# An exchange of partition quarters through DRAM by four scattered writes and one contiguous read, with new order tables

## The chip, the cores and the metric

The kernel runs on one core of a Trainium2 chip. The metric is the device time of one launch in microseconds (us), the median of several runs. The core's engines are TensorE (PE: matmuls and transposes), VectorE (DVE), ScalarE (ACT), GpSimd (POOL) and SyncE (SP), which here only issues transfers (DMAs). Each engine works through its own instructions in a fixed order and waits where an operand or a buffer isn't ready; whatever stands behind a waiting instruction on that engine waits too, transfers on SP's queue included.

## The reference

One layer of a hybrid decoder on x of 512 positions by 1,024 features, all in float32: a normalised input is projected, three head groups (a gated delta rule, a diagonal state-space mixer called S5, and differential attention) work on it, one projection joins them, and a gated MLP with a short convolution follows. The change concerns the transfers of the S5 group; the new orders concern all of it.

```python
h = rms_norm(x, attn_norm_w)
g_q, g_k, g_v, g_z, g_b, g_a, s_u, d_q, d_k, d_v = split_cols(h @ w_in, IN_SIZES)
o_gdn = gated_delta_chunked(l2norm(g_q), l2norm(g_k), g_v, beta, log_decay)   # 4 heads, chunks of 64
o_s5 = rms_norm(s5_mixer(s_u, ...), s5_norm_w)     # 32 groups, 64 complex states, scan over positions, GELU, GLU
o_diff = diff_attention(d_q, d_k, d_v, lam)        # 4 heads, two causal softmax maps each
x = x + concat([o_gdn * silu(g_z), o_s5, o_diff]) @ w_out
x = x + (silu(gate) * up) @ w_down                 # gate, up = causal_dwconv(rms_norm(x) @ w_up)
out = rms_norm(x, final_norm_w)
```

## The kernel before

The features lie on the 128 partitions in eight tiles, the positions along the row. A weight matrix comes as blocks of 256 KB (`wblock`, line 550): a transfer into `wraw`, a cast on ScalarE to the rounded part `whi` (line 566), a subtraction on VectorE to the rest `wlo`. There are three buffers of each, so the transfer of a block waits until the `wlo` of the block three before it is written. Every product is three matmuls (rounded by rounded, rounded by rest, rest by rounded; `mm3`), accumulated in one of two PSUM banks `acc`. A bank is free again when ScalarE or VectorE has copied the result out; for the values of the attention that is the copy `dv` (line 1252), one for each half of the positions.

The order of TensorE's work is written out by hand in a string. The orders of VectorE, ScalarE, GpSimd and the issuing queue are four tables of numbers (`SEQUENCE`), which `in_order` ties into chains: number k is the k-th instruction of that engine in the order in which the program creates them.

The S5 group works in four parts. For part i, `s5_in` computes the input `up`, and `swap` (line 691) exchanges quarters of the partitions with quarters of the row, so that `u4` holds 32 positions in each quarter of the partitions; `s5_back` makes the output `yu` (VectorE, with a GELU whose tanh is on ScalarE) and exchanges it back into `yf`. So there are eight exchanges, called u0 to u3 and y0 to y3 here. An exchange is one transfer that writes the tile (256 KB, rows of 2 KB) to a DRAM tile `m` as it is, and four transfers of 64 KB that read a quarter of the partitions each, in pieces of 512 B. `yh` (line 812, ScalarE) and `yl` (VectorE) split `yf` for a later product; they are not urgent themselves, but stand in their engines' orders among the weight casts.

Other names in what follows: `gg` (VectorE, line 269) is the log decay of the delta rule, `cs`, `ct`, `z`, `zt` are the rotations and sums around the S5 scan, `en`, `wn`, `d` and `ff` tables and small blocks for matmuls, `kq` and `thc` the short convolution and its SiLU for the delta rule, `t_`, `f_`, `xc`, `lct` the steps of its triangular inverse (each `f_` a transpose of 32 by 32 blocks on VectorE, copied to `ff` by ScalarE). In the attention `dsm` is the row maximum (a reduction, line 1309) and the sums, `pp` the two probability maps and their difference, `qa`, `ka`, `kl` split queries and keys.

Of the kernel before, what the change touches and what calls it, by code (L numbers as in the profile page):

```python
# [59 lines left out]
226 172 244 173 219 174 222 175 243 176 223 177 246 178 224 179 254 180 201 181 225 182 202 183 228 184 203 185 227  # L60
186 229 187 230 188 272 277 231 122 233 123-124 232 125 210-211 234 212 235 304 213-214 256 236 306 257 305 269 215
258 237 259-262 273 263 274 264 275 265 311 266 276 267 239 268 238 240 307 293 292 296 309 294 310 295 328 297 312
332 308 313 247 314 248 250 249 298 324 251 315 325 327 326 316 329 333 252 279 278 280-281 334 299 301 300 282 335
302 330 303 284 283 336 318-319 285 320 337 286 364 321-322 331 365 287 323 288 290 289 291 366 353 352 355-356 354
357 367 359 358 338-341 379 360 255 361-362 342 381 363 344 343 374 368 373 345 369 375 346 270 376-377 271 347 378
348 350 370 349 351 371 396 413 389 388 391 390 192 196 392 193 197 393 414 317 194 380 416 382 372 384 383 419 394
397 395 385-386 398-400 415 401-403 405 404 406-407 420 408-409 411 410 412 424-425 417 387 418 461 421 426 463 422
460 462 427-429 434 423 435 440 430-432 441 433 436-437 458 438-439 442 459 443 456 455 457 444-448 468 449-452 477
453 464 454 469 482 465 470 466 471 467 472 476 473-475 487 498 478-480 483 481 500 484 488 485 489 486 490 493
491-492 494 503 495-497 506 499 511 501-502 522 504-505 507 538 509 508 512 542 510 544 513 516 514-515 541 517-518  # L70
521 519-520 543 548 523-525 533 527 529 531 539 534 553 545 535 540 536 526 546 528 537 547 530 532 560 549-550 554
551 555-556 552 561 587 557 588 558-559 579 563 580-582 564 577 576 578 583 565 562 566-569 584 601 570 585-586
571-572 589 573 598 574 603 575 593 590 600 591 594 592 595 597 599 609 596 602 610 604 614 605-607 615 608 612-613
611 616 623 619 617-618 620-622 628 641 624-627 642 629-633 651 637-638 634 639 635-636 652 640 643 669 668 670 653
647 644 671 648 645 649 654 646 650 657-658 655-656 663 659 664 660-662 693 665-667 672 674 694 675 673 696 677-678
691 690 697 679 692 680-683 676 684 695 713 685-687 719 688-689 698-699 703-704 700-702 734 705 714 709-710 706 711
707-708 712 715 735 720-722 716-718 729 723 727-728 730 724-726 731-733 738 736 739-740 737 742 744 741 748 743 754
745-747 759 749-750 752 751 753 763 755 757 756 758 765 760-762 769 764 772 766 768 767 775 770 778 771 773 781 776
784 779 787 782 790 785 794 788 774 791 777 793 780 783 800 786 789 792 801 795 802 1121-1122 796-799 1123 810 1124
803 1125-1126 804 806 811 815 805 807 816 808 1127-1128 812 821-822 813 809 814 817 826 818-819 827 823 832 820  # L80
# [11 lines left out]
1110 1115 1112 1117 1114 1119 1116 1118 1120 1129-1147 1149 1148 1153 1150-1151 1154-1155 1152 1156-1158  # L92
""",
    "scalar": """
0-1 3 2 5 4 6-24 27 25 29 33 26 28 51 30 44 31 46 34-35 43 52 45 36 39 49 37 40 38 41-42 57 32 50 53 55-56 92 97
58-59 54 62-64 60 65-66 61 67 69-76 68 77-81 86-87 82-85 108 93-94 88-89 102-104 47 95 110 105-106 90 48 91 107 96
121 123 109 98 111-114 99-101 115-117 124-125 122 118 126 150-151 131-132 127-128 146 137-139 129 119 140 144 130
141 120 142 147 145 148-149 133-136 168 143 174 152-154 158 156 189 159 190-191 155 192 157 160-161 164 166 165 162
186 169 167 170-173 197-202 175 212 163 176 214 178 177 179 183 185 180 184 187 181 193-194 188 195-196 204-207 203
215 208-211 182 222-223 220 213 257 216 259 217 225 221 218 256 258 226 228 224 229 232 227 219 233 236 230 237 231  # L100
# [51 lines left out]
def hybrid_trunk(ctx: ExitStack, tc: tile.TileContext, I: dict, out: bass.AP):  # L152
    nc = tc.nc
# [19 lines left out]
    dma = nc.sync.dma_start  # L173
# [1666 lines left out]
```

## Time and profile before

| | us |
|---|---|
| Median of 3 runs | 829.7 (827.82 to 830.31) |
| Profiled execution | 831.47 |
| Span of its trace, first to last instruction | 829.3 |
| TensorE busy | 792.8 |
| VectorE busy | 561.9 |
| ScalarE busy | 430.8 |
| GpSimd busy | 104.4 |

The mean granted clock of TensorE is 0.972 of the full one. In a timeline row the first number is the start, the second the time from the start to the end of what the row merges (xN instructions, whose pipelined times overlap a little), then engine, line, operation, result and operands, and in brackets how long the engine had been idle and what released it. A line such as L182 or L263 is a helper's that issues all matmuls or all tensor operations, so the names of the tiles tell the places apart.

### The profile page before, as it was taken

The numbers are of one execution on the slowest core, as the hardware profiler recorded it, in microseconds if no ns is written. First come the engines' busy times: TensorE is split into PE (matmuls) and PEld (weight loads), VectorE is DVE, ScalarE is ACT, GpSimd is POOL, SyncE is SP. The second block draws the span as 40 slices with busy tenths as digits, with TensorE's granted clock in tenths as the row PEclk, the third lists the DMA queues.
The fourth block names the chain that finished last, engine by engine and source line by source line (L and its number), as shares of the span: only waits on it lengthen the run. The fifth ranks groups of instructions, "written<-read, shape, count | busy, mean of one in ns | idle before, by whom it ended". The sixth has DMA issues, their size and how long they took to land.

```text
span 829.3 us, 13695 instructions
## 1 busy us (share of the span) xinstructions
PE 792.8 (96%) x5004; PEld 653.9 (79%) x5004; DVE 561.9 (68%) x1159; ACT 430.8 (52%) x1001; POOL 104.4 (13%) x133
## 2 busy tenths in 40 slices
PE   6979989998999999999999999999999999999996
PEld 6868877986777878787777788788888888888885
DVE  8998898754757866548447976766557656657634
ACT  5266356644567966675547644344244334335423
POOL 5710000000001210010003211011001001001101
PEclk8998999998998999999989999999999999999998
DMA  6856453378383633341214532333333333333202
GB/s 158 102 94 51 92 77 87 61 111 61 81 45 53 44 67 72 94 70 55 84 44 125 182 100 83 107 102 90 101 90 101 102 89 102 95 96 100 78 1 102
DMA packets 133562, 71.58 MB, mean 86 GB/s; under 512 B 12766, under 2 KB 129784, under 8 KB 133496
## 3 DMA queue, kind: packets, MB, share of 16 engines
q1 hardware_dynamic: 133496, 70.72, 40.6%
q8 instruction: 39, 0.64, 0.3%
q14 instruction: 27, 0.22, 0.1%
HBM read 66.51 MB, written 4.19 MB: 85 GB/s over the span
## 4 chain that ended last, share of the span: by engine, by line
PE 74%; DVE 11%; DMA 6%; ACT 4%; issue 2%; POOL 1%; SPq 1%; POOLq 0%; DVEq 0%; ACTq 0%
PE acc L182 62%; PE gp L182 5%; PE sp L182 4%; DMA wraw<-in_w_in_dram 4%; DVE wlo L263 2%; DVE kq L269 1%; PE sp L185 1%; DVE z L263 1%; PE gp L185 1%; DMA yf<-swap 1%; ACT whi L566 1%; DVE ct L263 1%; DVE z L662 1%; ACT gm L1022 1%; DVE zt L263 0%
## 5 line engine op out<-in xcount | busy, mean ns | idle before, releaser
L566 ACT CAST whi<-wraw 128x512 fp32r<-128x512 f32 (+2 forms) x224 | 133.2, 597 | 169.1 <-PE acc L182 142.5
L182 PE MATMUL acc<-h,whi 128*128 128x512 f32 x704 | 217.7, 390 | 0.0
L263 DVE TENSOR_TENSOR wlo<-wraw,whi 128x512 fp32r<-128x512 f32 (+2 forms) x224 | 151.7, 680 | 55.7 <-ACT whi L566 49.9
L182 PE MATMUL acc<-hT,whi 128*128 128x512 f32 (+1 forms) x464 | 154.2, 409 | 4.7 <-ACT dv L1252 2.9
L182 PEld LDWEIGHTS acc<-h,whi 128*128 128x128 f32 x704 | 132.1, 188 | 28.6 <-DVE h L269 0.6
L182 PE MATMUL acc<-h,wlo 128*128 128x512 f32 x352 | 137.0, 390 | 0.0
L182 PEld LDWEIGHTS acc<-hT,whi 128*128 128x128 f32 x464 | 88.6, 198 | 20.6 <-ACT dv L1252 3.1
L182 PE MATMUL acc<-hT,wlo 128*128 128x512 f32 (+1 forms) x240 | 92.6, 398 | 0.0
L263 DVE TENSOR_TENSOR x<-x,acc 128x512 f32<-128x512 f32 (+1 forms) x65 | 44.0, 677 | 57.3 <-PE acc L182 57.3
L182 PEld LDWEIGHTS acc<-h,wlo 128*128 128x128 f32 x352 | 66.1, 188 | 14.0 <-DVE wlo L263 0.3
L269 DVE SCALAR_TENSOR_TENSOR ac<-us,rt,ac 128x511 f32<-128x511 f32 x88 | 65.9, 750 | 12.9 <-ACT ac L1719 11.5
L263 POOL TENSOR_TENSOR ac<-ac 128x512 f32<-128x512 f32 x22 | 35.6, 1619 | 280.5 <-DVE ac L269 161.3
L182 PE MATMUL acc<-ah,whi 128*128 128x512 f32 x144 | 57.6, 400 | 0.1
L182 PE MATMUL acc<-ah,wlo 128*128 128x512 f32 x144 | 56.5, 392 | 0.0
L182 PE MATMUL acc<-al,whi 128*128 128x512 f32 x144 | 56.0, 389 | 0.0
L401 POOL TENSOR_TENSOR rs<-ms,expo 128x4 f32<-128x4 f32 (+1 forms) x14 | 19.3, 1375 | 278.8 <-DVE ms L400 274.6
L182 PEld LDWEIGHTS acc<-hT,wlo 128*128 128x128 f32 x240 | 46.4, 198 | 7.5
L263 DVE TENSOR_TENSOR us<-acc,rb 128x512 f32<-128x512 f32 x44 | 30.3, 688 | 27.9 <-PE acc L182 27.9
L1719 ACT ACTIVATE ac<-us,rt 128x512 f32<-128x512 f32 x44 | 36.0, 817 | 21.5 <-DVE us L263 21.5
L263 DVE TENSOR_TENSOR al<-ac,ah 128x512 fp32r<-128x512 f32 x22 | 15.2, 691 | 28.1 <-ACT ah L1733 27.5
L182 PEld LDWEIGHTS acc<-ah,whi 128*128 128x128 f32 x144 | 27.1, 188 | 6.7 <-issue 1.1
L1733 ACT CAST ah<-ac 128x512 fp32r<-128x512 f32 x22 | 13.7, 622 | 35.8 <-POOL ac L263 35.8
(567 smaller groups left out, 1404.2 us busy)
## 6 DMA issues: line engine op xcount, KB each, us to landing
wraw<-in_ffn_w_up_dram SPq DMA_DIRECT2D x88, 256.0 KB
wraw<-in_w_in_dram SPq DMA_DIRECT2D x64, 256.0 KB
wraw<-in_ffn_w_down_dram SPq DMA_DIRECT2D x32, 256.0 KB
wraw<-in_w_out_dram SPq DMA_DIRECT2D x24, 128.0 KB
xt<-in_x_dram SPq DMA_DIRECT2D x4, 512.0 KB
xj<-in_x_dram SPq DMA_DIRECT2D x8, 256.0 KB
wraw<-in_w_out_dram SPq DMA_DIRECT2D x8, 256.0 KB
lwraw<-in_ffn_w_down_dram SPq DMA_DIRECT2D x8, 256.0 KB
```

The lines of the kernel that those rows point to most:

```text
L182: pe(T.matmul(o, l, r, start=start, stop=stop))
L185: pe(T.transpose(o, i, ident_))
L263: e.tensor_tensor(o, a, b, op=op)
L269: e.scalar_tensor_tensor(o, a, s, b, op0=op0, op1=op1, **kw)
L401: ins = G.tensor_tensor(rs[:, :n], ms[:, :n], expo[:, :n], op=ALU.pow)
L566: S.copy(hi[:, :n], raw[:, :n])
L662: V.tensor_tensor_scan(zf[j], rr, zf[j], 0.0, ALU.mult, ALU.add)
L1022: S.activation(gm[:, n, :], m_ge, AF.Copy, scale=gp[:, n, h : h + 1])
L1719: S.activation(a, us, AF.Identity, scale=fcw(2, f), bias=fcb(f))
L1733: S.copy(ah[:, j, :], up)
```

## The change

`swap` writes four times, each time a quarter of the partitions into its place in every one of the 128 rows of `m` (pieces of 512 B), and then reads the whole of `m` in one transfer of 256 KB with rows of 2 KB. It is still five transfers per exchange, on the same queue. The four tables of `SEQUENCE` are new; TensorE's order is unchanged. Every line behind `swap` is one line further down in the new file.

```diff
     "sync": """
-9-12 14-15 13 16-17 19-23 32-33 40 34 57 41 58 35 42 59 36 38 43 37 39 44 26-29 60 24-25 30-31 61-62 47 52 63-64
+9-12 14-15 13 16-17 19-23 32-33 40 34 41 57-58 35 42 59 36 38 43 37 39 44 26-29 60 24-25 30-31 61-62 47-50 63 52-53
...
     def swap(o, x, n):
 
         m = dr.tile([P, 4, P], F32, name=f"swap{n}")
-        dma(m, x)
-        for b in range(4):
-            dma(o[32 * b : 32 * b + 32], m.rearrange("(a j) b c -> b j a c", j=32)[b])
+        v = m.rearrange("(b j) a c -> a j b c", j=32)
+        for a in range(4):
+            nc.sync.dma_start(v[a], x[32 * a : 32 * a + 32])
+        nc.sync.dma_start(o, m)
```

The issuing queue around the exchange y0 (`swap4`, from `yu` to `yf`) and u2 (`swap2`, from `up` to `u4`), before:

```order
L694 DMA swap4_1321<-yu_1319 128x512
L564 DMA wraw_1608<-in_w_in_dram 128x4x128
L696 DMA yf_124<-swap4_1321 32x4x128 x4
L694 DMA swap2_1452<-up_1449 128x512
L564 DMA wraw_1626<-in_w_in_dram 128x4x128
L696 DMA u4_1450<-swap2_1452 32x4x128 x4
L564 DMA wraw_1715<-in_w_in_dram 128x4x128
```

and now:

```order
L696 DMA swap4_1321<-yu_1319 32x4x128 x4
L564 DMA wraw_1608<-in_w_in_dram 128x4x128
L697 DMA yf_124<-swap4_1321 128x512
L696 DMA swap2_1452<-up_1449 32x4x128 x2
L564 DMA wraw_1626<-in_w_in_dram 128x4x128
L696 DMA swap2_1452<-up_1449 32x4x128 x2
L564 DMA wraw_1715<-in_w_in_dram 128x4x128
L697 DMA u4_1450<-swap2_1452 128x512
```

The four reads of y0 are one, behind the same weight block; u2 has its four writes around a weight block, and its read behind one more block.

ScalarE from the copies `wt` on, in the stretch that holds the first copy of `dv`, before:

```order
L742 COPY wt_1561<-sp_1560 128x512
L742 COPY wt_1568<-sp_1567 128x512
L1160 COPY ff_538<-f__1437 32x4x32
L773 COPY d00_120<-sp_1574 128x4x32
L775 COPY d00_120<-sp_1574 32x4x32 x2
L1252 COPY dv0_1458<-acc_1459 128x512
L790 COPY enx_116<-en_1329 64x32x16
```

and now:

```order
L743 COPY wt_1561<-sp_1560 128x512
L743 COPY wt_1568<-sp_1567 128x512
L1253 COPY dv0_1458<-acc_1459 128x512
L774 COPY d00_120<-sp_1574 128x4x32
L776 COPY d00_120<-sp_1574 32x4x32 x2
L566 CAST whi_1716<-wraw_1715 128x512
L1253 COPY dv0_1458<-acc_1460 128x512
```

The copy of `acc_1459` stands ahead of the `d00` copies, and the `ff` copy has gone from here (it now stands some ten rows further back).

VectorE in the attention's third and fourth blocks of rows, with a step of the triangular inverse (`xc`, `t__3441`, `f__3442`) between, before:

```order
L1110 STREAM_TRANSPOSE xc_3443<-lct_3436 128x128
L1309 TENSOR_REDUCE dsm_3545<-sp2_3546 128x2
L263 TENSOR_TENSOR xc_3443<-xc_3443,levs_511 128x128
L263 TENSOR_TENSOR kl0_3652<-dqk_2502,ka0_3646 64x512
L263 TENSOR_TENSOR t__3441<-ic_531,xc_3443 128x128
L263 TENSOR_TENSOR wlo_3706<-wraw_3704,whi_3705 128x512
L1110 STREAM_TRANSPOSE f__3442<-t__3441 128x128
L263 TENSOR_TENSOR xc_3584<-gp_3567,levs_511 128x128
L1314 RECIPROCAL dsm_3545<-dsm_3545 128x2
```

and now:

```order
L1111 STREAM_TRANSPOSE xc_3443<-lct_3436 128x128
L263 TENSOR_TENSOR xc_3443<-xc_3443,levs_511 128x128
L263 TENSOR_TENSOR t__3441<-ic_531,xc_3443 128x128
L1310 TENSOR_REDUCE dsm_3545<-sp2_3546 128x2
L1111 STREAM_TRANSPOSE f__3442<-t__3441 128x128
L263 TENSOR_TENSOR xc_3584<-gp_3567,levs_511 128x128
L263 TENSOR_TENSOR kl0_3652<-dqk_2502,ka0_3646 64x512
L263 TENSOR_TENSOR qa0_3644<-dqk_2502,qa0_3644 64x512
L263 TENSOR_TENSOR t__3610<-t__3441,gp_3593 128x128
L263 TENSOR_TENSOR qa1_3645<-dqk_2502,qa1_3645 64x512
L1315 RECIPROCAL dsm_3545<-dsm_3545 128x2
```

The reduction and `kl0` stand behind `t__3441`, and `wlo_3706` further back; two `qa` rows have come in.

The tables also move these: on VectorE two products `z` go behind `gg`, one `wlo` comes ahead of it; two sums `z` go behind `yu` of y1; two `qa` rows and one `wlo` come ahead of `yu` of y3. On ScalarE the tanh of y3 goes behind two `qa` casts and a weight cast. On the issuing queue one more weight block stands ahead of the exchange y3.

## Rows read from the trace of the kernel before

**Rows 1.** The page's first part: engine, busy us, share of the span, instructions

```profile
PE 792.8 (96%) x5004; PEld 653.9 (79%) x5004; DVE 561.9 (68%) x1159; ACT 430.8 (52%) x1001; POOL 104.4 (13%) x133
```

**Rows 2.** The page's fourth part: the chain that ended last, by engine

```profile
PE 74%; DVE 11%; DMA 6%; ACT 4%; issue 2%; POOL 1%; SPq 1%; POOLq 0%; DVEq 0%; ACTq 0%
```

**Rows 3.** TensorE's waits, 0 to 300 us: line, releaser, total, times, longest

```profile
PE gp L185 <- DVE kq L269: 3.5, 1, 3.5
PE gp L182 <- DVE gg L269: 3.4, 1, 3.4
PE acc L182 <- ACT dv L1252: 2.9, 1, 2.9
...
PE gp L182 <- DVE t__3441 L263: 2.2, 1, 2.2
...
PE sp L182 <- DVE yu L269: 1.0, 1, 1.0
```

**Rows 4.** TensorE's timeline at 113 us: start, length, instruction, idle before and releaser

```profile
113.70 0.99 PE L182 MATMUL acc<-hT,whi 128*128 128x512 f32 x2 [2.94 <-ACT dv L1252]
...
117.45 0.62 PE L182 MATMUL acc<-hT,whi 128*128 128x512 f32 x2
```

**Rows 5.** ScalarE's timeline, 101 to 114 us

```profile
101.63 0.63 ACT L812 ACTIVATE yh<-yf 128x512 fp32r<-128x512 f32 x1 [4.10 <-DMA yf<-swap]
...
111.89 0.30 ACT L1160 COPY ff<-f__1437 32x128 f32<-32x128 f32 x1 [4.81 <-DVE f__1437 L1110]
...
113.06 0.58 ACT L1252 COPY dv<-acc 128x512 f32<-128x512 f32 x1
```

**Rows 6.** VectorE's timeline at three places

```profile
59.87 0.68 DVE L263 TENSOR_TENSOR z<-sp,cs 128x512 f32<-128x512 f32 x1
...
102.80 0.69 DVE L263 TENSOR_TENSOR wlo<-wraw,whi 128x512 fp32r<-128x512 f32 x1 [2.62 <-ACT whi L566]
...
136.59 1.28 DVE L263 TENSOR_TENSOR z<-z,zt 128x512 f32<-128x512 f32 x2
```

**Rows 7.** Stretches: their length, each engine's busy time, clock, DMA share, GB/s

```profile
120.00:140.00 20.00, 18.30 (x145) 15.32 (x143) 19.71 (x39) 12.06 (x29) 0.00 (x0) 1.00 0.33 81
300.00:829.00 529.00, 518.25 (x2845) 421.48 (x2843) 325.85 (x554) 254.02 (x527) 58.64 (x43) 0.99 0.32 90
```

**Rows 8.** The issuing queue's timeline at the y0 and y3 exchanges

```profile
93.41 0.34 SPq L694 DMA_DIRECT2D swap<-yu  x1
...
95.41 1.75 SPq L696 DMA_DIRECT2D yf<-swap  x4
...
174.08 0.34 SPq L694 DMA_DIRECT2D swap<-yu  x1
...
177.97 2.71 SPq L696 DMA_DIRECT2D yf<-swap  x3
```

**Rows 9.** ScalarE's timeline, 186 to 293 us

```profile
186.15 0.63 ACT L812 ACTIVATE yh<-yf 128x512 fp32r<-128x512 f32 x1 [2.85 <-DMA yf<-swap]
...
197.16 0.62 ACT L566 CAST whi<-wraw 128x512 fp32r<-128x512 f32 x1 [4.21 <-DMA wraw<-in_w_in_dram]
...
292.44 1.25 ACT L1278 CAST qa<-dqk 64x512 fp32r<-64x512 f32 x2
```

**Rows 10.** Two more stretches, columns as in rows 7

```profile
97.00:101.00 4.00, 4.00 (x36) 4.00 (x34) 3.18 (x6) 0.52 (x2) 0.00 (x0) 1.00 0.85 182
188.00:200.00 12.00, 9.19 (x47) 7.62 (x45) 7.08 (x12) 3.70 (x8) 0.00 (x0) 0.97 0.92 40
```

**Rows 11.** VectorE's timeline, 289 to 295 us

```profile
289.21 1.23 DVE L1309 TENSOR_REDUCE dsm<-sp 128x2 f32<-128x1024 f32 x1
...
291.84 0.28 DVE L263 TENSOR_TENSOR t__3441<-ic,xc 128x128 f32<-128x128 f32 x1
...
294.27 0.75 DVE L269 SCALAR_TENSOR_TENSOR pp<-pp,dsm,pp 128x512 f32<-128x512 f32 x1
```

**Rows 12.** TensorE's timeline at 296 us

```profile
296.45 0.66 PE L185 MATMUL sp<-ident,pp 128*128 128x128 f32 x4
```

More of the change, by code (lines that the diff above doesn't have):

```diff
@@ L60 @@
[L60 to L74, printed above, removed]
@@ new lines @@
+114-115 142 116 155 139 117-118 143 119 140 147 144 152 126 148 220 145 167 146 149-150 156 127 153-154 168 157-158
+120 161 159-160 121 190-191 205 195 204 207-208 206 209 169 162 170 242 171 163-164 198 221 199 216 200 217 245 218
+226 172 241 173 219 174 244 175 243 176 246 177 222 178 201 179 223 180 254 181 224 182 202 183 272 184 225 185 203
+186 228 187 227 188 229-230 277 231 233 232 122 234 123-124 210 125 235 211 256 304 212 257 306 269 305 258 213
+259-262 214 263 236 273 264 274 265 275 266 311 267 276 268 215 237 239 307 238 240 309 293 310 292 296 294 312 295
@@ new lines @@
+426 463 421 460 462 427 422 428-429 434 423 435 440 430-432 441 433 436-437 458 438-439 442 459 443 456 455 457
+444-448 468 449-452 477 453 464 454 469 482 465 470 466 471 467 472 476 473-475 487 498 478-480 483 481 500 484-485
+488 486 489-490 493 491-492 494 503 495-497 506 499 511 501-502 522 504-505 507 538 509 508 512 542 510 513-516 541
+543-544 521 517-520 548 523-525 533 527 529 531 539 526 545 534 553 535 540 536 528 546 530 547 532 549 560 550 537
+551 555-556 554 552 561 557 587 558-559 588 579 563 580-583 564 562 576-577 565 578 566-569 584 570 585 601 571 586
@@ L107 @@
[L107 to L108 removed]
+0-1 3 5 2 4 6-24 27 25 29 33 26 28 51 30 44 31 46 34-36 43 52 45 39 49 37 40 38 41-42 57 32 50 92 53 55-56 97 58-59
+62-64 54 60 65-66 61 67 69-76 68 77-81 86-89 82-85 108 93-94 102-106 110 95 90 107 91 96 121 47-48 123 109 111-114
+98-101 115-117 124-125 122 118 126 131 150-151 132 127-129 137-139 144 130 119 140-141 120 145 142 146-149 133-134
@@ new lines @@
+168 143 135-136 174 152-154 158 156 189-190 159 191-192 155 157 160-161 186 166-167 162 169-170 164 171 165 172-173
+212 197 175 198-202 176 163 214 178 177 179 183 185 180 184 187 181 193-194 188 195-196 204-207 203 215 208-211 182
+222-223 220 213 257 216 259 225 221 217 256 258 226 218 228 224 229 232 227 219 233 236 230 237 231 234 253 235
+238-241 246-247 242-245 248-249 252 254 262 250-251 268 255 271 260-261 265 263-264 266-267 275 283 269 274 270 286
+272-273 278-281 276-277 289 282 297-298 293-294 292 284 295-296 285 308 287-288 319 290-291 299-301 329 305 302 306
@@ new lines @@
+303 332 311 304 312 307 309 313 310 314 334 331 333 315-316 352 317 353 318 344 354 320 355 321-322 326 323 327 347
+335 330 324 336 325 342 337 356-357 343 361-362 358-359 338-341 363 345 364 328 348-349 393 365-368 346 360 350-351
+370-373 396 374-375 386 376-378 384-385 387 379-381 388 369 391 389-390 392 408 382 394 383 395 404 406 399 403 405
+397-398 400 415 401-402 419 407 409-410 420 411-414 416 426 417 427 418 421-425 429 432 461-462 457-460 443 428
+430-431 446 435 433-434 436 452 437 440-441 438-439 444-445 453 442 489 491 449 488 490 447 455 450 448 456 451 454
```

54 lines of the change are left out of this document (23 added, 31 removed).

## Prediction

> **What bounds the kernel now.** I read the page's engine table first: TensorE is busy 792.8 of 829.3 us [rows 1]. The chain of work that ended last lies on TensorE for 74%, on VectorE for 11% and on transfers for 6% [rows 2]. So a change that leaves the matmuls alone, as this one does (their order is word for word the same), can win only the 36.5 us in which TensorE stands, and what its clock loses after a stand. The table of TensorE's waits in the first 300 us says whom it waits for: `kq` 3.5, `gg` 3.4, `dv` 2.9, `t__3441` 2.2, `yu` 1.0 [rows 3]. From 300 us on it works 518.3 of 529 us [rows 7], and a microsecond won earlier reaches the end whole.
>
> The second view is the timeline at three of these waits. At 113.70 TensorE has stood 2.94 us for ScalarE's copy of `dv`, and its pairs of matmuls then take 0.99 us or a little more; from 117.45 they take 0.62 [rows 4]. That is the lower of the two clock levels for some 3.7 us, and costs another 1.4 to 1.6. ScalarE tells why `dv` is late: its `yh` waited 4.10 us for the exchange's transfer, `ff` waited 4.81 us for VectorE's `f__1437`, and `dv` stands behind `ff` in ScalarE's order [rows 5]. VectorE in turn stood 2.62 us for the weight cast that is queued behind `yh` [rows 6]. From 120 to 140 us VectorE works 19.71 of 20 us [rows 7]: there it is the bound, and TensorE's 1.0 on `yu` belongs to it.
>
> **The change part by part.** The sum is made against the profiled execution of 831.47 us (span 829.3, 2.2 around it), and the difference is then put on the median of 829.7.
>
> *The order ahead of `gg` on VectorE.* Two products `z` of 0.68 us each, of which about 0.6 counts because neighbours overlap (59.87 is the second [rows 6]), go behind `gg`, one `wlo` comes ahead of it. That is 0.6 us off the wait of 3.4 [rows 3]. The products themselves come later on an engine that is nearly full until 140 us, so between 0 and 0.6 of it reaches that point. I take −0.4.
>
> *The y0 exchange and what is queued behind it.* Before, the write is issued at 93.41, the first of the four reads at 95.41, 2.00 us later, and the issues of the four take 1.75 us [rows 8]. The data is used at 101.63 [rows 5], about 4.5 us after the last read's issue at about 97.1. Now four writes take some 1.4 us to issue (four of 0.34, the issue time of the row at 93.41), the last is complete 2.0 later if it behaves as the one write did, and one read follows at about 96.4 to 96.8. How long it takes no row shows: the nearest are 2.0 us (the contiguous write of the same bytes) and 4.5 us (the last of the four reads, with `u2`'s write and a weight block behind it). It lands between 98.4 and 101.3; I take 99.6, nearer the write, since both move whole rows of 2 KB. `wlo` starts 1.17 behind `yh` as before (102.80 − 101.63 [rows 5, 6]), so at 100.8 instead of 102.80. VectorE's work ahead of it sums to the same (one `z` goes behind it, one `cs` comes ahead), so its own earliest is 102.80 − 2.62 = 100.18. Gain on VectorE: 2.0, with ends of 0.3 and 2.6.
>
> *The `dv` copy on ScalarE* now stands right behind the two `wt` copies and ahead of every `d` copy, with the `ff` copies far behind. It no longer hangs on `f__1437`, so the 2.94 and the 1.5 of slow clock, some 4.4 us in all, leave this place. They don't all reach the end. What is late next is VectorE at `yu` of y1 (TensorE waited 1.0 for it already). VectorE comes there earlier by the 2.0 above and by the two sums `z` (1.28, at 136.59 [rows 6]) that now stand behind `yu`. So by 139 us TensorE gains 2.0 + 1.3 = **3.3**, not the 5.4 that are open to it. Ends: 1.6 if the read lands late, 4.5 if other small stands of VectorE close up too.
>
> *The y3 exchange.* Here the new orders put two `qa` rows and one `wlo` ahead of `yu`, and on ScalarE the tanh behind two casts and a weight cast: some 2.6 us later (VectorE rows of 0.7, ScalarE rows of 0.62 as at 197.16 [rows 9]). Before, the write went out at 174.08 and the last three reads from 177.97 on [rows 8], after one weight block more had left; `yh` started at 186.15 after 2.85 of waiting, and the next casts, and with them the buffers of later weight blocks, stand behind it [rows 9]. Those later blocks come slowly: from 188 to 200 the transfer engines are 92% busy at 40 GB/s [rows 10], and the cast at 197.16 that waited 4.21 us for such a block [rows 9] is what makes `kq` late and TensorE wait 3.5. So each microsecond by which `yh` moves moves that wait. Now: writes from about 176.7 to 178.1, complete about 3 later, one read at about 181 instead of a last one at about 180.3, one weight block between writes and read as before. A single read against four: −1 to +2, and I take **+0.5**.
>
> *`t__3441` on VectorE.* The reduction of 1.23 us and a `kl` row move from ahead of it to behind it; between the reduction's start and `t__3441`'s lie 2.63 us [rows 11], of which one small row stays. All of the 2.2 goes. But `pp` now stands behind two `qa` rows and a `wlo`, and ScalarE's exponentials behind two `qa` casts (1.25 [rows 9]). Before, `pp` ended at 295.02 [rows 11] and TensorE took it at 296.45 [rows 12], 1.4 later; now I get an end of about 295.7 against a need at about 294.6. A new wait of about 1.0 to 1.4 takes the place of the old one: net **−0.8**, with ends −2.2 and +0.3.
>
> Everything else (rows that change places while TensorE is full, tables of the start, three other exchanges whose users have slack of some microseconds) I cost at 0: the cover is the full TensorE between the waits of [rows 3]. If it is gone, each costs the 0.6 of one row.
>
> Sum: −0.4 − 3.3 + 0.5 − 0.8 = **−4.0**, so 827.5 for a profiled execution, and 829.7 − 4.0 = **825.7** for the median.
>
> **The rivals.**
> *The new exchange is no faster* (it doesn't do what it says): the read has to wait for the slowest of four writes, and lands at 101.3. Then VectorE gains 0.3 instead of 2.0 and the sum is −2.3: 827.4. For it speaks that the number of transfers, five, and the bytes are the same; against it that the two legs are of equal length only if a contiguous read is as slow as a scattered one, and the 2.00 beside the 4.5 says otherwise. The Trainium skill, "DMA: Bandwidth & Descriptors", section "Anatomy of one DMA", gives each transfer a fixed cost of about 2.0 us, most of it the receipt of the last byte, heaviest in HBM, plus its bytes over the fabric's rate. By that rule a whole and a quarter in series cost the same in either order, and the result is this rival's 827.4. The write's 2.00 us agrees with the rule, while the reads' 4.5 does not.
>
> *What is won is lost at y3*: the read of y3 lands 3 us later than before. The sum becomes −0.4 − 3.3 + 3.0 − 0.8 = −1.5: 828.2, no difference. For it speaks that `yu` is 2.6 us later; against it that the block queued between is the same one and one read replaces four.
>
> *Slower: scattered writes crawl.* No row shows a write in pieces of 512 B; weight blocks that are read in such pieces move at 40 GB/s from 188 to 200 [rows 10]. At that rate 256 KB take 6.5 us instead of the write's 2.0: +4.5 in each exchange. At y0 `yh` then comes at about 104, and VectorE loses 2.3 instead of winning 2.0; at y3 the wait for `kq` grows by 4.5 to 5. Sum: −0.4 + 2.3 − 1.3 + 5.0 − 0.8 = +4.8: 834.5. It decides once the four writes take longer than about 5 us from first issue to the read's issue. Against it: around the y0 reads, from 97 to 101 us, where nearly all is read in pieces of 512 B too, the same engines moved 182 GB/s [rows 10].
>
> **How the numbers follow.** The forecast (825.7) gets 0.60, the exchange that is no faster 0.15, the loss at y3 0.12, crawling writes 0.13. A difference of 0.3%, 2.5 us, is about what a measurement of this kernel can tell from no change. The first case lies beyond it, the two middle ones (827.4 and 828.2) within it, the last is slower: 0.60, 0.27, 0.13. The ends of the terms add up to −8.3 and +0.7, but not all fall on one side; with the middle rivals inside and the last one left out, the range is 821.5 to 829.8.
>
> **What would show it.** In the profile after: TensorE's wait for `dv` near 113 gone and its clock whole there; VectorE's 2.62 before `wlo` near 100 under 1; the wait for `yu` of y1 still there or grown to 1 to 2 (VectorE the bound); the wait for `kq` near 196 at 3 to 5; the wait for `t__3441` gone and one of about 1 for `pp` a few us later; the y0 read used 2 us earlier relative to its `yu`. I am wrong if the time from the first of four writes to the read is well over 3.5 us, if `dv` is still waited for, or if a new wait of over 2 us stands after 200 us.

## The result, and the profile after

The changed kernel takes 817.1 us (median of 4 runs, 814.98 to 822.96) against 829.1 for the kernel before on the same chip: a ratio of 0.9876 with an interval of 0.9835 to 0.9916 (an estimate over all runs; the two medians alone give 0.9855). The difference of the medians is 12.0 us where 4.0 were forecast, and 817.1 lies outside the range of 821.5 to 829.8. The direction was right and the amount wrong.

The profiled execution took 822.96 us and its span is 820.8, the slowest of the four; a second profiled execution of the same program (e1 below) has a span of 813.9. Both are needed to read the result. The first part of the page after (of the first of the two) answers to [rows 1]:

```profile
PE 788.9 (96%) x5004; PEld 649.6 (79%) x5004; DVE 560.9 (68%) x1159; ACT 430.8 (52%) x1001; POOL 103.1 (13%) x133
```

TensorE is busy 3.9 us less with the same 5,004 matmuls, so some of the gain is clock (the matmuls themselves run faster), not idle time. The view of stretches splits the two. Its columns are those of [rows 7]: the third number is TensorE's busy time, the one before the DMA share its granted clock. Of the kernel before (from 300 us on see [rows 7]; the stretch from 152 to 188 us, with TensorE full and the clock whole in both kernels, is left out):

```profile
0.00:20.00 20.00, 13.23 (x71) 12.20 (x72) 16.43 (x67) 11.53 (x26) 10.47 (x27) 0.88 0.71 163
20.00:106.00 86.00, 79.95 (x715) 67.89 (x715) 79.44 (x247) 42.80 (x116) 20.55 (x46) 0.95 0.59 84
106.00:122.00 16.00, 13.06 (x79) 11.54 (x78) 14.86 (x31) 8.78 (x23) 0.00 (x0) 0.89 0.68 84
122.00:152.00 30.00, 28.30 (x202) 24.32 (x201) 24.23 (x55) 17.44 (x43) 0.00 (x0) 0.94 0.36 79
...
188.00:212.00 24.00, 20.52 (x91) 16.97 (x89) 12.64 (x31) 10.42 (x34) 1.64 (x1) 0.86 0.77 67
212.00:300.00 88.00, 83.58 (x787) 67.26 (x786) 63.75 (x140) 64.81 (x187) 9.87 (x12) 0.96 0.51 54
```

and of the changed kernel:

```profile
0.00:20.00 20.00, 13.93 (x79) 13.43 (x80) 17.05 (x67) 11.56 (x26) 11.31 (x27) 0.83 0.71 163
20.00:106.00 86.00, 79.43 (x705) 66.94 (x704) 78.75 (x246) 41.88 (x113) 18.55 (x46) 0.94 0.64 83
106.00:122.00 16.00, 16.00 (x104) 14.13 (x103) 15.86 (x34) 11.08 (x28) 0.00 (x0) 1.00 0.70 92
122.00:152.00 30.00, 27.12 (x222) 23.89 (x220) 26.13 (x60) 20.32 (x54) 0.00 (x0) 1.00 0.39 82
...
188.00:212.00 24.00, 21.09 (x195) 17.09 (x196) 15.22 (x41) 13.04 (x45) 1.64 (x1) 1.00 0.70 82
212.00:300.00 88.00, 84.82 (x699) 68.03 (x698) 62.67 (x132) 65.67 (x183) 11.34 (x13) 0.96 0.51 53
300.00:820.00 520.00, 510.92 (x2809) 415.19 (x2807) 320.99 (x548) 249.55 (x518) 57.01 (x42) 0.99 0.32 91
```

Length less busy time, summed over the rows, is TensorE's idle time: 36 us before, 31 after. Length times what the clock lacks of 1.00 is the clock's loss: 22.4 before (1.8 of it from 106 to 122, 1.8 from there to 152, 3.4 from 188 to 212) and 17.3 after, with the clock whole from 106 to 212. So about 5 us left the idle time, close to the forecast sum, and another 5 the clock, for which the forecast had 1.5 in one place. (Where TensorE stands at the lower clock, both sums count the time.) In the second execution the same sums give 28 and 12. Over stretches of 4 us, where the rounding of the clock counts less, the clock's loss is 17.4 in the first and 10.1 in the second (table below): of the 7 us by which the second is shorter, with the same program, most is clock.

**The three places of the prediction.** At y0, after: the issuing queue (the name behind the instruction is what it writes), then ScalarE, VectorE and TensorE.

```profile
93.41 1.78 SPq L696 DMA_DIRECT2D swap<-yu  x4
...
96.59 0.34 SPq L697 DMA_DIRECT2D yf<-swap  x1
...
101.75 0.63 ACT L813 ACTIVATE yh<-yf 128x512 fp32r<-128x512 f32 x1 [3.96 <-DMA yf<-swap]
...
109.62 0.59 ACT L1253 COPY dv<-acc 128x512 f32<-128x512 f32 x1 [1.15 <-PE acc L182]
...
102.92 0.69 DVE L263 TENSOR_TENSOR wlo<-wraw,whi 128x512 fp32r<-128x512 f32 x1 [1.89 <-ACT whi L566]
...
110.86 0.63 PE L182 MATMUL acc<-hT,whi 128*128 128x512 f32 x2
```

The read goes out 3.18 us behind the first write (2.00 before [rows 8]) and its data is used 5.16 us later: `yh` at 101.75 and `wlo` at 102.92 are where they were, at 101.63 and 102.80 [rows 5, 6], from the same first issue at 93.41. The exchange is not faster. The wait for `dv` is gone all the same, and the matmuls behind run at 0.63 from the start, where [rows 4] had 0.99.

At y3, after (issuing queue, ScalarE, TensorE):

```profile
171.72 1.77 SPq L696 DMA_DIRECT2D swap<-yu  x4
...
177.21 0.34 SPq L697 DMA_DIRECT2D yf<-swap  x1
...
180.86 0.63 ACT L813 ACTIVATE yh<-yf 128x512 fp32r<-128x512 f32 x1 [3.09 <-DMA yf<-swap]
...
188.91 0.70 PE L182 MATMUL acc<-hT,whi 128*128 128x512 f32 x2 [1.19 <-DVE kq L269]
...
196.00 0.66 PE L185 MATMUL gp<-ident,kq 128*128 128x128 f32 x4 [1.85 <-DVE kq L269]
```

Here the write leg is 5.49 us, the read leg 3.65. `yh` comes 5.3 us earlier than at 186.15 [rows 9], while TensorE is 4.5 ahead. The one wait of 3.5 for `kq` [rows 3] has become two of 1.19 and 1.85, and the half clock behind it is gone. Which half of the change does this, e3 shows (below).

At `t__3441`, after (VectorE, TensorE):

```profile
282.68 0.29 DVE L263 TENSOR_TENSOR t__3441<-ic,xc 128x128 f32<-128x128 f32 x1
282.89 1.22 DVE L1310 TENSOR_REDUCE dsm<-sp 128x2 f32<-128x1024 f32 x1
...
287.90 0.74 DVE L269 SCALAR_TENSOR_TENSOR pp<-pp,dsm,pp 128x512 f32<-128x512 f32 x1
...
288.80 0.63 PE L185 MATMUL sp<-ident,pp 128*128 128x128 f32 x4 [1.04 <-DVE pp L269]
```

The wait of 2.2 is gone and one of 1.04 for `pp` stands in its place, as forecast (1.0 to 1.4).

### The profile page after: what moved, and what is told of

Same layout as the page of the kernel before. It is cut to its first block, busy times and chain, and to the rows that moved or that the text cites. A ratio compares the mean times of both kernels' runs of the same rounds, so it can differ in the third digit from the quotient of the medians.

```text
span 820.8 us, 13688 instructions
## 1 busy us (share of the span) xinstructions
PE 788.9 (96%) x5004; PEld 649.6 (79%) x5004; DVE 560.9 (68%) x1159; ACT 430.8 (52%) x1001; POOL 103.1 (13%) x133
## 4 chain that ended last, share of the span: by engine, by line
PE 77%; DVE 8%; DMA 7%; ACT 4%; issue 2%; SPq 1%; POOL 1%; POOLq 0%; DVEq 0%; ACTq 0%
PE acc L182 65%; PE gp L182 5%; PE sp L182 5%; DMA wraw<-in_w_in_dram 4%; PE sp L185 1%; DVE wlo L263 1%; PE gp L185 1%; DVE kq L269 1%; DMA wraw<-in_w_out_dram 1%; DMA yf<-swap 1%; DMA swap<-yu 1%; ACT whi L566 1%; PE acc L1608 0%; SPq L696 0%; ACT yh L884 0%
## 5 line engine op out<-in xcount | busy, mean ns | idle before, releaser
L182 PE MATMUL acc<-hT,whi 128*128 128x512 f32 (+1 forms) x464 | 150.0, 400 | 1.2 <-DVE kq L269 1.2
L182 PEld LDWEIGHTS acc<-hT,whi 128*128 128x128 f32 x464 | 86.1, 193 | 16.1 <-issue 1.6
L182 PE MATMUL acc<-hT,wlo 128*128 128x512 f32 (+1 forms) x240 | 90.9, 390 | 0.0
L269 DVE SCALAR_TENSOR_TENSOR ac<-us,rt,ac 128x511 f32<-128x511 f32 x88 | 65.9, 750 | 13.1 <-ACT ac L1720 11.7
L263 DVE TENSOR_TENSOR al<-ac,ah 128x512 fp32r<-128x512 f32 x22 | 15.2, 691 | 29.9 <-ACT ah L1734 29.3
```

The costliest lines, as they stand in the source:

```text
L182: pe(T.matmul(o, l, r, start=start, stop=stop))
L263: e.tensor_tensor(o, a, b, op=op)
L269: e.scalar_tensor_tensor(o, a, s, b, op0=op0, op1=op1, **kw)
```

## The experiments

Each kernel ran in several rounds beside the kernel before on its chip; medians of before differed between the chips (825.6 to 829.1), so kernels are compared by the ratio. Idle time and clock loss are of the one profiled execution, summed over stretches of 4 us as above (before, so summed: 36.5 and 23.2). The last columns are where TensorE stands against the trace of before when it starts the matmul that before starts at 119, 150, 206 and 300 us. That trace is of a long execution (831.47 us): most of the others are already 1 to 3 us ahead of it at 105 us, e4 too (2.7), whose edit acts only behind that, and the two executions of one program in the first two rows differ by 2 us at 119 and by 5 at 300. So it is the change of the lead from one column to the next that is read, not its size.

| kernel | median, us | ratio, 95% interval | idle | clock loss | 119 | 150 | 206 | 300 |
|---|---|---|---|---|---|---|---|---|
| changed | 817.1 | 0.9876 [0.9835, 0.9916] | 31.9 | 17.4 | −4.5 | −4.5 | −7.2 | −7.7 |
| e1, the same again | 816.9 | 0.9872 [0.9827, 0.9917] | 29.3 | 10.1 | −6.6 | −5.9 | −9.4 | −12.6 |
| e2, exchange alone | 824.0 | 0.9978 [0.9950, 1.0007] | 34.4 | 16.0 | −3.7 | −3.2 | −7.2 | −6.8 |
| e3, tables alone | 818.7 | 0.9876 [0.9824, 0.9929] | 28.8 | 15.4 | −5.9 | −6.4 | −6.6 | −9.0 |
| e4, `dv` alone | 826.3 | 0.9983 [0.9955, 1.0011] | 34.8 | 19.5 | −7.5 | −2.7 | −3.9 | −3.9 |
| e8, `dv` and `yu` | 827.3 | 1.0001 [0.9978, 1.0025] | 33.7 | 21.1 | −5.1 | −1.0 | −1.8 | −1.6 |
| e7, e3 without `dv` | 823.2 | 0.9962 [0.9945, 0.9980] | 31.9 | 17.2 | −0.9 | −3.1 | −4.8 | −6.5 |
| e5, new orders to 139 us | 826.9 | 1.0017 [0.9991, 1.0043] | 33.1 | 21.5 | −6.4 | −1.2 | −0.9 | −1.8 |
| e6, new orders from 139 us | 825.2 | 0.9989 [0.9962, 1.0015] | 32.8 | 15.8 | −2.1 | −2.1 | −1.4 | −4.1 |
| e12, e5 and `r` | 826.2 | 0.9983 [0.9957, 1.0010] | 35.6 | 14.3 | −6.8 | −3.2 | −3.8 | −6.6 |
| e14, e12 and `vn` | 827.4 | 0.9989 [0.9968, 1.0009] | 35.0 | 14.2 | −6.5 | −2.2 | −2.4 | −5.2 |
| e10, e5 and the rows around `r` | 818.0 | 0.9909 [0.9876, 0.9942] | 31.2 | 13.3 | −7.6 | −8.5 | −9.4 | −10.3 |
| e11, new exchange in y1 and y3 only | 817.8 | 0.9875 [0.9836, 0.9915] | 29.2 | 12.7 | −7.1 | −6.4 | −9.9 | −9.9 |

### Which half of the change carries it: e1, e2, e3

e1 is the changed kernel once more: the times repeat (816.1 to 820.1), the expectation that its stages agree with those of the first trace within 1 us fell. e2 has only the new `swap`:

```diff
-        dma(m, x)
-        for b in range(4):
-            dma(o[32 * b : 32 * b + 32], m.rearrange("(a j) b c -> b j a c", j=32)[b])
+        v = m.rearrange("(b j) a c -> a j b c", j=32)
+        for a in range(4):
+            nc.sync.dma_start(v[a], x[32 * a : 32 * a + 32])
+        nc.sync.dma_start(o, m)
```

with the tables of before, and on the issuing queue the four writes where the write stood and the read where the first read stood. e3 has the new tables and undoes the same lines (the minus lines are kept).

> The changed kernel once more, for a second trace and more times. The first trace had TensorE at half clock for some microseconds after a wait of 3.4 us on pl at 44.5 us, and its time, 823, was the longest of its four (815 to 823). If that is chance of an execution (theory: the start of the kernel and the clock vary, the rest doesn't), this run gives 815 to 823 again, and in its trace the stages from 62 us on differ from the first trace by less than 1 us, while the wait on pl may be between 1 and 3.5 us. Rival: the stage after 200 us varies too, so the stand on kq (1.9 us) and the clock behind it differ by more than 1 us.

> The new exchange alone, with the orders of before; on the issuing queue the four writes stand where the one write stood, and the read where the first of the four reads stood. Theory (the gain lies in the orders): within 2 us of before, 827 to 830; y0's yu to yh 8 to 9 us as in both traces (8.9 and 9.05), TensorE's wait for dv still 2 to 3 us. Rival (the exchange gives it): 3 us or more below before, 822 to 826, above all by an earlier yh of y3 (12.8 us behind yu before, 9.9 after) and so a shorter wait for kq.

> The new orders with the old exchange; the one write stands where the first of the four writes stands, the four reads where the one read stands. Theory (orders): 8 to 12 us below before, within 2 us of the changed kernel, 816 to 821; no wait for dv, none for t__3441, one of about 1 us for pp. Rival (exchange): at least 3 us above the changed kernel, with the wait for kq near 196 at 3 us or more and half clock behind it.

The tables alone give the whole ratio of 0.9876; the exchange alone gives −0.2%, with an interval from −0.5% to +0.1%. The time from the start of `yu` to the start of `yh`, exchange by exchange, says why. In y0 to y3 it is 8.89, 8.25, 6.73 and 12.79 us before, 9.05, 6.98, 7.62 and 9.85 after, 8.97, 7.77, 7.17 and 10.15 in e2, and 8.56, 7.67, 6.57 and 10.27 in e3. With the new exchange (after and e2) y0 and y2 become longer by 0.1 to 0.9 us, y1 shorter by 0.5 to 1.3. Only y3 is shorter by 2.5 to 2.9, by the new exchange alone as well as by the new tables alone, so the two don't add. (In y1 of before and e2 and in y3 of e2 `yh` started without a wait for the transfer, so these times are upper ends.) The legs of y0 in e2 (issuing queue, then ScalarE) are those of the changed kernel, 3.18 and 5.11:

```profile
91.25 1.78 SPq L696 DMA_DIRECT2D swap<-yu  x4
...
94.43 0.34 SPq L697 DMA_DIRECT2D yf<-swap  x1
...
99.54 0.63 ACT L813 ACTIVATE yh<-yf 128x512 fp32r<-128x512 f32 x1 [4.18 <-DMA yf<-swap]
```

At one place the traces do tell the exchanges apart: at `kq`, behind y3. In e3, with the old one (issuing queue, TensorE, the stretch behind it):

```profile
176.07 1.75 SPq L696 DMA_DIRECT2D yf<-swap  x4
177.92 11.66 SPq L564 DMA_DIRECT2D wraw<-in_w_in_dram  x5
...
188.74 1.19 PE L182 MATMUL acc<-hT,whi 128*128 128x512 f32 x2 [2.87 <-DVE kq L269]
...
188.00:192.00 4.00, 3.27 (x8) 2.63 (x9) 3.29 (x5) 1.78 (x3) 0.00 (x0) 0.50 0.97 38
```

and on the changed kernel's issuing queue, behind the one read at 177.21:

```profile
177.65 12.11 SPq L564 DMA_DIRECT2D wraw<-in_w_in_dram  x5
```

With four reads the next weight block leaves 1.85 us after the first of them, with one read 0.44 after it, and 6.64 us behind the start of `yu` instead of 8.76. In all ten traces with the old exchange in y3 TensorE stands 2.65 to 4.51 us for `kq` in one piece, and the clock falls. In the four with the new one (changed, e1, e2, e11) no such stand is over 1.87, and the clock stays whole there. From the matmul at 186 us of before to the one at 206, TensorE gains 2.7 to 4.1 us with the new exchange and −0.7 to 1.7 with the old. So the exchange is worth some 2 to 4 us at this place; the medians differ by 1.8 (e1 and e3) and 1.7 (before and e2), which so few runs can't tell from nothing. The bulk of the gain is the tables'.

### The `dv` copy alone: e4, e8, e7

e4 moves one number of ScalarE's table, so that the first copy of `dv` stands right behind the copies `wt`; e8 also puts `yu` of y1 ahead of the two sums `z` on VectorE; e7 is e3 with the copy of `dv` behind `ff` (146) and three copies `d` again, the order of before, for which both `dv` and `ff` move.

```diff
 e4, ScalarE
-... 150-151 131-132 127-128 146 137-139 129 119 140 144 130
+... 150-151 131-132 127-129 146 137-139 119 140 144 130
 e8, VectorE, besides
-348 350 370 349 351 371 396 413
+348 350 370-371 349 351 396 413
 e7, ScalarE, against e3
-... 150-151 132 127-129 137-139 144 130 ... 146-149
+... 150-151 132 127-128 146 137-139 129 144 130 ... 147-149
```

> The kernel before with one edit: in ScalarE's order the copy of the first half of dv stands right behind the two copies wt, ahead of ff and the d copies. The prediction's step said that VectorE at yu of y1 is the next bound, so that this copy alone is worth some 0 to 1 us by 139 us (VectorE is not made faster): 828 to 829.5. Rival, from the trace after, where TensorE came 4.4 us earlier although VectorE reached that yu only 1.7 us earlier: the copy alone is worth 2 to 4.5 us: 824.5 to 827.

> The kernel before with two edits: the copy of dv ahead of ff and the d copies, and on VectorE the two sums z behind yu of y1 instead of ahead of it. The prediction's step: VectorE's 1.3 us ahead of yu are what kept the copy alone from paying, so 1.3 us more than the copy alone: about 2.7 below before. Rival: other rows of VectorE hold yu and its neighbours back as well (the wait for yu stays at 1 us or more), and the result is that of the copy alone, within 1.5 of before.

> All the new orders with the old exchange, except that on ScalarE ff and three d copies stand ahead of the copy of the first half of dv again, as before. Theory: the wait for dv comes back with 2 to 3 us and the clock behind it, and since VectorE is no longer the bound with the new orders, most of it reaches the end: 3 to 5 us above the new orders alone (819), 822 to 824. Rival (the prediction's step: VectorE at yu of y1 is the bound, the copy alone moves nothing): within 1.5 us of 819.

With `dv` alone TensorE is 7.5 us ahead at 119 and 2.7 at 150; 2.7 it had at 105 already, so all of the 4.8 won at `dv` is lost again. Its waits in between, in e4:

```profile
128.39 0.65 PE L182 MATMUL gp<-ff,xm 64*64 64x64 f32 x8 [1.80 <-issue]
...
131.76 0.49 PE L182 MATMUL gp<-vt,ff 128*128 128x128 f32 x2 [0.89 <-ACT ff L1191]
...
134.52 3.59 PE L182 MATMUL sp<-cmx,wnx 128*128 128x32 f32 x16 [1.40 <-DVE yu L269]
```

Three waits, 4.1 us in all, give it back, and the clock falls in the last of them (0.50 from 134 to 138 us): the group at 134.52 takes 3.59 us, against 1.97 in e5, e12 and the changed kernel. Moving `yu` ahead of the two sums (e8) wins nothing measurable: the wait for it is 0.99, as in before, and 1.29 and 0.90 stand ahead of it; VectorE itself waits 0.70 there for ScalarE's `ge`. So `dv` alone is worth nothing measurable. But with all the other new orders in place its order with `ff` and `d` is worth 0.9% by the ratios (0.9962 against 0.9876, whose intervals don't meet), 4.5 us by the medians. e7 shows the stand again, in TensorE's timeline and, columns as in [rows 7], in the stretch behind it:

```profile
111.85 1.22 PE L182 MATMUL acc<-hT,whi 128*128 128x512 f32 x2 [3.51 <-ACT dv L1252]
```

```profile
112.00:116.00 4.00, 4.00 (x10) 3.13 (x11) 3.10 (x5) 2.44 (x6) 0.00 (x0) 0.50 0.44 39
```

TensorE stands 3.51 us, and its clock is at the lower level for all of the next 4 us.

### Which stretch: e5, e6, and what stands behind the cut: e10, e12, e14

e5 takes the new orders up to about 139 us and the old ones behind, e6 the reverse; both have the old exchange. The tables of GpSimd and of the issuing queue are the new ones as a whole in e5 and the old ones in e6. The cut on VectorE falls just ahead of the rows that e10 and e12 then change (380 is `r`, a step of the delta rule; 414 `sp`, for which the copies `d` on ScalarE wait; 389 `ct`; 388, 390, 391 and 393 `en`; 317 `yl`; 416 a `wlo`; 382 the delta rule's `state`). On ScalarE 175 is `vn`, which follows `r`, 197 to 202 are the copies `d`, 212 a weight cast.

```diff
 e5, VectorE: first 376 numbers new, these and the rest old
+... 349 351 396 413 389 388 391 390 192 196 392 193 197 393 414 317 194 380 416 382
 e6, VectorE: first 376 numbers old, these and the rest new
+... 349 351 371 396 413 389 380 414 388 416 390-391 382 392 192 196 393 383-384 193 197 317
 e12, VectorE, against e5
-413 389 388 391 390 192 196 392 193 197 393 414 317 194 380 416 382
+413 380 389 388 391 390 192 196 392 193 197 393 414 317 194 416 382
 e14, ScalarE, against e12
-197-202 175 212 163 176
+175 197-202 212 163 176
 e10, VectorE and ScalarE, against e5
-413 389 388 391 390 192 196 392 193 197 393 414 317 194 380 416 382
+413 389 380 414 388 416 390-391 382 392 192 196 393 383-384 193 197 317
-197-202 175 212 163 176
+212 197 175 198-202 176 163
```

> The new orders of all engines up to about 139 us (VectorE up to the row behind yu of y1, ScalarE up to the same place, GpSimd and the issuing queue whole), the orders of before behind that, the old exchange. Theory (several short stands, each with the clock behind it, add up): about half of the gain of the new orders, 4 to 6 us below before: no wait for dv, but 2.2 for t__3441 and about 3.5 for kq near 196 with the clock down behind it. Rival (the stages depend on each other: what is won early is eaten at kq, where a late transfer sets the time): within 2 us of before.

> The orders of before up to about 139 us, the new ones of VectorE and ScalarE behind that, the old exchange. Theory (the parts add up): 4 to 6 us below before, the rest of the gain: dv waited for as before (about 3 us and the lower clock behind), no wait for t__3441, about 1 for pp, no clock loss at 250. Rival: late orders bring only the 0.8 that the prediction gave t__3441: 828 or within 1.5 us of before.

> As the early half of the new orders, with the boundary a little later on VectorE and ScalarE (up to the tanh of y2), so that r of the delta rule (VectorE) stands ten rows earlier as in the changed kernel; the old exchange. In the early half alone TensorE waited 3.8 us for r at 140 us, just where the gain of dv was lost. Theory (r is the next bound once dv and yu have moved): the wait for r falls under 1 us, TensorE is 4 to 5 us ahead of its own time at 105 us when it comes to 146 us of before, and 3 to 5 us of it reach the end: 822 to 825. Rival (what is won early is eaten at kq near 196, where a late weight block sets the time): ahead at 146 us, but the wait for kq grows to 6 us or more and the end is within 1.5 us of before.

> The kernel of e5 (new orders up to about 139 us, old exchange) with one instruction moved: r_1896 of the delta rule stands on VectorE where the new table has it, directly behind ct_1970, ahead of sp_1875, yl and en. The rows that e10 also moved (nine more on VectorE, eleven on ScalarE) stay as in e5. Theory, that the place of r alone carries the difference between e5 (827) and e10 (818): TensorE's wait for r near 141 us falls from 3.77 to under 1 us, the half clock behind it goes, and the median is 818 to 822. Rival, that what stands beside r (the rows en, yl and the tanh on ScalarE) carries it: another wait of 2 us or more takes the place at 138 to 147 us, and the median stays within 2 us of e5's 827.

> The kernel of e12 with one more number moved: on ScalarE vn, the next step of the delta rule behind r, stands ahead of the six d copies instead of behind them (in e12 it waited there for those copies, the copies for VectorE's sp, and TensorE 2.99 us for vn at 140.81). Everything else as in e12. Theory, that the chain r on VectorE and vn on ScalarE has to be ahead on both engines and is what e10 did: the wait for vn is gone, no half clock at 140 to 146, TensorE keeps its lead of about 8 us from 137 on, and the median falls from 826 to 818 to 822. Rival, that the slack is taken by what stands behind (the d copies 0.4 later, then yh and the weight casts, and the wait for kq of 3.8 near 192 that e12 shows): the lead at 146 is there, but the wait for kq grows to 5 or more with half clock behind it, and the median stays at 824 to 827.

Neither half of the tables gives anything that can be measured (+0.2% and −0.1%), both together 1.24%. The trace of e5 shows what eats the first half (VectorE, then TensorE):

```profile
139.16 0.32 DVE L263 TENSOR_TENSOR sp<-sp,dd 32x128 f32<-32x128 f32 x1
...
140.31 0.35 DVE L269 SCALAR_TENSOR_TENSOR r<-gp,neg,vt 128x128 f32<-128x128 f32 x1
...
140.72 0.80 PE L182 MATMUL gp<-r,ff 128*128 128x128 f32 x2 [3.77 <-DVE r L269]
```

and the stretch behind it has the lower clock throughout:

```profile
140.00:144.00 4.00, 3.28 (x10) 2.80 (x11) 1.33 (x4) 2.48 (x8) 0.00 (x0) 0.50 0.05 14
```

With the stand for `dv` gone, TensorE comes to `r` at 136.95 and waits 3.77 us for it behind the rows `en`, `sp` and `yl`. In the kernel before those rows stood there too, hidden by the late `dv`: TensorE came 7 us later, and had no wait (VectorE, then TensorE):

```profile
142.98 0.35 DVE L269 SCALAR_TENSOR_TENSOR r<-gp,neg,vt 128x128 f32<-128x128 f32 x1
...
144.02 0.63 PE L182 MATMUL gp<-r,ff 128*128 128x128 f32 x2
```

e10, which puts some ten rows of VectorE and as many of ScalarE where the new tables have them, waits 0.58 there, and 826.9 becomes 818.0, more than was expected of it. e6 has these rows in their new places as well, with the late `dv`, and gives nothing measurable: neither they nor the orders up to 139 us pay alone.

My reading at that point, that `r` alone does it, fell, and the rival of e12 held. e12 moves `r` and nothing else (to one row ahead of its place in the new table), and TensorE stands for the next link `vn` instead (TensorE, then ScalarE):

```profile
140.81 0.49 PE L182 MATMUL gp<-vn,kt 128*128 128x128 f32 x2 [2.99 <-ACT vn L1207]
...
138.74 0.27 ACT L773 COPY d<-sp 128x128 f32<-128x128 f32 x1 [3.96 <-DVE sp L263]
```

`vn` starts at 140.39, behind the copies `d`, which wait 3.96 us for VectorE's `sp` behind the same `en` rows. e14 moves `vn` ahead of them, and the stand is at the link after that, `state`, which VectorE has behind a `wlo` that waits for ScalarE (TensorE, then VectorE):

```profile
143.03 0.79 PE L182 MATMUL gp<-state,kq 128*128 128x128 f32 x2 [3.08 <-DVE state L269]
...
141.91 0.69 DVE L263 TENSOR_TENSOR wlo<-wraw,whi 128x512 fp32r<-128x512 f32 x1 [1.40 <-ACT whi L566]
142.63 0.35 DVE L269 SCALAR_TENSOR_TENSOR state<-state,ed,gp 128x128 f32<-128x128 f32 x1
```

3.77, 2.99, 3.08: the stand moves along the chain and keeps most of its size. Both kernels lose 3.6 and 4.3 us of their lead there (table, 119 to 150), nearly all of the 4.8 won at `dv`, and are not faster than before by a measurable amount. So neither the theory of e12 nor that of e14 holds: it takes more of the rows that e10 moves. My reading is `sp` ahead of `en`, which brings the copies `d`, the weight cast and `yh` on ScalarE forward together with `r`, `vn` and `state`. In e10 (VectorE, then ScalarE):

```profile
135.24 0.34 DVE L269 SCALAR_TENSOR_TENSOR r<-gp,neg,vt 128x128 f32<-128x128 f32 x1
135.62 0.32 DVE L263 TENSOR_TENSOR sp<-sp,dd 32x128 f32<-32x128 f32 x1
...
135.97 0.27 ACT L773 COPY d<-sp 128x128 f32<-128x128 f32 x1 [0.72 <-DVE sp L263]
```

TensorE then keeps its lead (−7.6 at 119, −8.5 at 150). That `sp` is the row that is needed beside `r` and `vn` is read from these waits and not shown: e10 also has `wlo` (416) and `state` (382) ahead of `yl`, and on ScalarE the weight cast ahead of the copies `d`, and none of them was run alone.

### A mixture: e11

e11 has the new tables, and the new exchange only in y1 and y3, whose transfers stand on the issuing queue as in the changed kernel (against e3):

```diff
+        if n in (5, 7):
+            v = m.rearrange("(b j) a c -> a j b c", j=32)
+            for a in range(4):
+                dma(v[a], x[32 * a : 32 * a + 32])
+            dma(o, m)
+            return
         dma(m, x)
```

> The new orders, with the new exchange in y1 and y3 only and the old one in the other six (in the traces so far the new one brings yh 0.3 to 1 us later behind yu in y0 and y2, and 0.5 to 1 earlier in y1 and y3). Theory: the y0 and y2 waits fall by 0.5 each, hidden behind other work; within 1.5 us of the changed kernel (817). Rival: 2 us or more below it, under 815.

0.9875 is what the changed kernel and e3 give. The one mixture that was run is not faster than the change as it stands.

## Why the prediction was wrong

**What bounds the kernel** held: TensorE's idle time and clock loss are nearly all that moved. What remains of the span is 770 to 775 us in all 14 traces, whose spans go from 814 to 829.

**The order ahead of `gg`** can't be judged: the wait is 1.7 in the changed kernel's profile and 3.3 in e1, the same program.

**The y0 exchange** failed, as a step: the read was to land at 99.6 at a cost of about 3 us, and took 5.16. The choice between 2.0 and 4.5 went to the wrong end, since the length of the rows did not decide it. The write leg was right (read out at 96.59, forecast 96.4 to 96.8). VectorE's wait ahead of `wlo` fell only from 2.62 to 1.89, not under 1, and `yf` is used 9.05 us behind its `yu` (8.89 before), not 2 us earlier. This is the rival *no faster*, on the exchange; the time that it gave, 827.4, was wrong because the exchange was not what carried the change. The Trainium skill, "DMA: Bandwidth & Descriptors", section "Anatomy of one DMA", by which either order costs the same, came out right in that, to 0.1 and 0.4 us in y0 and y2 of e2. The section is written for transfers that GpSimd issues, and its price doesn't fit these of SyncE: an estimate by it is 2.6 us for 256 KB, where the write took 2.00 and the read 5.16. The scattered writes did not crawl: 3.18 us to the read in y0, though 5.49 in y3. There the place makes it, not the scatter: e3's one contiguous write took 6.20 (169.87 to 176.07) with the same tables, and the four scattered ones 3.09 with the old tables (e2).

**The `dv` copy and what is late next** is the term that was mis-sized. The stand went as said, with its clock: from 105 to 119 us TensorE gains 4.8 and 4.7 in the two profiled executions. I then let VectorE at `yu` take back all but 3.3, and that bound was wrong. With `dv` alone all is lost again (e4), as the step has it, but not to VectorE's rows ahead of `yu`: with the two sums out of the way e8 is no better. In the change too much was taken back: VectorE is as full as before (19.84 of the 20 us from 115.5), but TensorE never waits for `yu` and leads by 4.5 and 5.9 at 150 us. The give-back hung on rows that I costed at 0 under "everything else", the order of `r`, `sp` and `en` on VectorE and of `vn` and `d` on ScalarE. Their cover was the late `dv` itself; once it is gone they are worth 3 to 4 us of standing plus the clock behind it (e5, e12, e14), and the new tables move them exactly there. The prediction gave the price "0.6 of one row" for a lost cover; the runs show a whole group of rows at once.

**The y3 exchange** had the wrong sign: +0.5 forecast, and TensorE gains 2.7 and 3.5 us from 186 to 206 in the two executions. `yh` came 0.8 earlier against TensorE instead of later. But the step that each microsecond of `yh` moves the wait for `kq` by as much failed too: in e3 `yh` is 0.4 earlier against TensorE, and the wait is still 2.87, with the clock down. The sum left out that four reads hold the queue longer than one, ahead of the weight blocks, and it did not have the clock behind the wait for `kq` at all. Of the kernel before and the changed one, two stretches each:

```profile
198.00:202.00 4.00, 1.33 (x5) 1.25 (x6) 1.86 (x3) 2.29 (x12) 0.00 (x0) 0.67 0.99 59
202.00:206.00 4.00, 4.00 (x11) 3.12 (x10) 0.17 (x1) 2.30 (x12) 1.64 (x1) 0.50 0.61 108
```

```profile
194.00:198.00 4.00, 2.15 (x13) 1.74 (x12) 1.26 (x3) 3.41 (x20) 0.00 (x0) 1.00 0.94 100
198.00:202.00 4.00, 4.00 (x20) 3.29 (x19) 2.30 (x11) 1.85 (x5) 1.64 (x1) 1.00 0.55 83
```

Before, the clock goes to its lower level in the stand of 3.48 us, and TensorE then works at half speed from 200.67 to about 206: by these two rows the clock's loss is 3.3 (1.3 and 2.0), of which some 0.7 falls in the stand itself; with the next row some 2.7 us of work are lost, three quarters of the wait. After the 1.85 of the changed kernel it stays whole. I counted that price behind `dv` (1.5) and nowhere else, though the rows for `kq` were open to me. Over both profiled executions idle time fell by 4.6 and 7.2, the clock's loss by 5.8 and 13.1 (the two overlap where TensorE stands at the lower clock, so they don't add up exactly); in the second a part of that is chance, since falls near 250 and 414 us of before are missing there and not in the first.

**`t__3441`** was right: 2.2 gone, 1.04 in its place, −0.7 to −1.0 between the two against −0.8.

Against the execution for which the sum was made, the first profiled one is 8.5 us shorter (831.47 to 822.96) and not 4.0: TensorE's lead grows by 4.8 from 105 to 150 us (3.3 forecast) and by 2.7 at `kq` (−0.5 forecast). The y3 term is the larger miss, the `dv` term the other.

So the rivals were placed at the speed of the exchange, whose worth alone is 0.2% (0.5% at the end of its interval), while the question was which rows of the tables are late next. That the change nevertheless came out faster, as forecast, is in part luck: the tables gave what the y0 exchange was to give.

**What stays open.** e10, without the new orders behind 139 us, has 0.9909, all of them 0.9876 (e3): the intervals overlap, so what the later orders add beyond e10 is not settled, and e6 shows nothing for them alone. Which rows beside `r` and `vn` it takes was not run, and the 2 to 4 us of the exchange at `kq` are read from traces; no median shows them. Nor is it settled why the clock falls in one execution and not in another of the same program (below).

## What to carry to other kernels

A row of work that costs nothing today is covered by something; before a wait is taken away, read along the next stretch, on every engine, what was hidden behind it, and move the whole group: moved one at a time, the stand here just passed to the next link (3.77, 2.99, 3.08 us). Parts of a planned order may have no price alone: here neither half is worth anything measurable, and both 1.2%. A stand of TensorE of about 3.5 us cost up to 1.8 times its length here (3.48 and 3.51, each with some 2.7 us of work lost to the clock behind it), while two of 1.19 and 1.85 cost only themselves; each one in the profile should be listed with the granted clock behind it before a sum is made.

## What the hardware showed

- From 20 us on, the clock's falls cost 1.7 or 3.4 us each in these traces (summed over stretches of 2 us, with the time in which TensorE stands anyway, and without the fall at the very end): 18 us in all in the kernel before, 12 in the changed one, 7 in its second execution. The second execution lacks the falls that the first has near 44, 242 and 406 us and has two of its own, with nothing changed in the program, and the times of the four runs spread over 8 us. The Trainium skill, "TensorE: Matmul & The Clock Gate", section "Part 1: The HAM clock gate", says that the point at which the clock changes is not tied to the kernel's start and varies from run to run; the two executions agree with it.
- A contiguous read of 256 KB took 5.16 us in y0 and 3.65 in y3, four scattered writes 3.18 and 5.49 to the read's issue. One contiguous write took 2.00 in y0 before, and 6.20 in y3 with the new tables (e3): the same transfer differs more between two places than the two kinds differ at y3.
